# The extra rows of an expert in pieces: the products behind their own branches, set between the steps of the main products

## The chip, the cores and the metric

The kernel runs on one core of a Trainium2 chip. The metric is the device time of one execution in microseconds (us). The engines are TensorE (PE in the profile, with PEld for its weight loads and PEq for its sequencer), VectorE (DVE), ScalarE (ACT), GpSimd (POOL) and SyncE (SP); DMA queues bring in the weights.

## The reference, cut to what matters

One decoder layer for 1024 tokens of width 1024: a mixer of three branches, a LayerNorm, and then a mixture of 16 experts, of which each token uses two. The change touches only the experts:

```python
D_MODEL = 1024
SEQ = 1024
N_EXPERTS = 16
TOP_K = 2
D_EXPERT = 512
...
# for every expert e and the tokens that the router gave it
h = silu(x @ w1[e]) * (x @ w3[e])      # 1024 -> 512
y = h @ w2[e]                          # 512 -> 1024
# weighted by the router and added to the token's row
```

With 1024 tokens and two experts each, an expert has 128 tokens on average, and some have more.

## The kernel before, in words

The first 1380 us of the span are the mixer and the router. The experts follow, one after the other, in a loop that is unrolled in the program. An expert has a **main part**: its first 128 tokens, one per partition. Their rows are gathered (`fetch`, tile xg), transposed on PE (`turn_a`: tile pxg, then ACT copies it to xgH and DVE makes xgL), multiplied by w1 and w3 in eight contraction steps (`layer1`, `mm_pair`, L1580, tiles ph), put through silu (`act`: ACT's tanh and two DVE operations make mhh), transposed (`turn2`: phT, mhH on ACT, mhL on DVE) and multiplied by w2 in four contraction steps (`layer2`, L1580, tiles py). ACT scales the result (mo, L1812) and POOL adds it to the rows in memory. Each weight tile of 128 rows and 1024 columns is split into two parts before it is used: a copy on ACT (L1634) and a subtraction on DVE (L1635), 12 such splits for an expert. A split is planned at the end of every step (`ws.step`), which also frees buffers and starts further loads.

The tokens above 128 are the **extra rows**, in groups m = 0 to 3 of 32. A value that is loaded from the router's counts (`count_of`, L1698) decides which groups there are. Each use of PE for them stands in a nest of four branches (`per_part`): the first group is computed when the count is over 128, the second, inside the first, when it is over 160, and so on. There are four stages with such a nest on PE: `part_x` transposes the gathered extra rows (then ACT copies them: xmT), `part_1` is the product with w1 and w3 (all eight contraction steps, 32 matmuls for a group, which the profile shows as 64), `part_act` is silu (mhm on ACT, two operations on DVE, no branch), `part_h` transposes (then ACT copies: hmT), `part_2` is the product with w2 (16 matmuls, shown as 32), and `part_y` multiplies by the router's weight on DVE (mom, no branch) and adds to memory from POOL. xmT, hmT, mhm and mom are made for all groups in every expert, whether it has extra rows or not. The stages write and read one tile `bank` in PSUM, whose half 0:256 of a group takes part_1's result and hT, and whose half 256:512 takes xT and part_2's result. The extra rows' products use the weight tiles as they were loaded, before the split, so that the loaded tiles can be given back (`ws.dropped`) only after them.

In the kernel before, a nest of part_1 or part_2 has a label, and a hint instruction some steps ahead of it (`ahead`, L1713) gives PE's sequencer the address that the branch will go to.

The order on PE, DVE and ACT is that in which the program is written. In the loop over experts e and steps c = 0 to 11, the steps 0 to 7 are layer1 of expert e, the steps 8 to 11 layer2 of expert e-1; after each step come the stages that a table (`AT`, `AT0` for the first expert, `LAST` for the last two) names for this step, and then `ws.step`. In a row (2, "part_1", 0) the numbers are the step and the expert counted from e.

## Time and profile before

| | us |
|---|---|
| median of three runs | 1901.77 (1892.07 to 1903.71) |
| the profiled execution | 1905.58 |
| its span | 1903.7 |
| experts in it, from about 1385 to 1864 us | 479 |

In a row of the trace a time in brackets is the idle time of the engine ahead of the row and what released it. "issue" is idle time for which the profile shows no wait, "PEq L1703" an instruction of PE's sequencer on the line of the branches. Consecutive instructions with the same operands are one row with their count.

### The profile page before, as it was taken

The page shows a single profiled execution, that of the slowest core. Times are in us where ns is not written, and L with a number is a line of the kernel's source. Part 1 is how long each engine was busy: PE and PEld are TensorE (multiplying, and loading weights), DVE is VectorE, ACT ScalarE, POOL GpSimd, SP SyncE. Part 2 cuts the span into 40 slices and gives each one's busy share as a digit, 9 for nine tenths or more (in the row PEclk, how much of TensorE's full clock was granted, in tenths as well). Part 3 has the DMA queues.
Part 4 walks back from the last instruction along what each step waited for, and adds up shares of the span by engine and source line. Part 5 has one row for each costly group of instructions (what it writes and reads, how often), then busy time and mean ns, then how long its engine had stood idle before and what let it go on. Part 6 is the DMA issues. An engine that isn't in the chain of part 4 may idle for free. (4 is left out here: it accounts for less than half of the span.)

```text
span 1903.7 us, 28756 instructions
## 1 busy us (share of the span) xinstructions
PE 1707.9 (90%) x10550; PEld 1433.5 (75%) x10550; DVE 1147.4 (60%) x2108; ACT 693.7 (36%) x1157; POOL 426.8 (22%) x434
## 2 busy tenths in 40 slices
PE   6996999999999999999999999999557978899782
PEld 5975988899998888888777778899545656677551
DVE  7699645544454442534476756735854547899666
ACT  6311322212212222435344532312133436688553
POOL 3186021113211103542110100000142213111115
PEclk9998999999999999999999999999779989999886
DMA  5232534233423233543200255482566768999835
GB/s 174 89 110 111 175 104 123 92 118 91 117 86 98 79 108 113 164 128 106 90 19 18 72 175 191 144 202 101 215 142 204 218 193 254 334 339 360 269 96 200
DMA packets 225790, 286.52 MB, mean 151 GB/s; under 512 B 48494, under 2 KB 153960, under 8 KB 225608
## 3 DMA queue, kind: packets, MB, share of 16 engines
q1 hardware_dynamic: 216936, 259.10, 42.2%
q0 software_dynamic: 8672, 24.94, 5.2%
q8 instruction: 120, 1.97, 0.4%
q14 instruction: 62, 0.51, 0.1%
HBM read 214.81 MB, written 69.17 MB: 149 GB/s over the span
## 5 line engine op out<-in xcount | busy, mean ns | idle before, releaser
L365 PE MATMUL psp<-xH,wh 128*128 128x512 f32 x704 | 286.3, 407 | 18.8 <-ACT ci L519 18.8
L366 PE MATMUL psp<-xL,wh 128*128 128x512 f32 x704 | 275.9, 392 | 3.8 <-DVE xL L234 2.3
L367 PE MATMUL psp<-xH,wl 128*128 128x512 f32 x704 | 277.2, 394 | 0.0
L365 PEld LDWEIGHTS psp<-xH,wh 128*128 128x128 f32 x704 | 133.3, 189 | 44.5 <-ACT ci L519 20.1
L365 PE MATMUL psp<-wh,xH 128*128 128x256 f32 (+1 forms) x576 | 166.2, 288 | 0.0
L367 PE MATMUL psp<-wh,xL 128*128 128x256 f32 (+1 forms) x576 | 162.9, 283 | 0.0
L366 PE MATMUL psp<-wl,xH 128*128 128x256 f32 (+1 forms) x576 | 162.9, 283 | 0.0
L366 PEld LDWEIGHTS psp<-xL,wh 128*128 128x128 f32 x704 | 133.4, 190 | 30.6 <-DVE xL L234 2.9
L367 PEld LDWEIGHTS psp<-xH,wl 128*128 128x128 f32 x704 | 132.8, 189 | 29.5
L1580 PE MATMUL ph<-wl,xgH 128*128 128x512 f32 x274 | 90.7, 440 | 32.0 <-issue 20.8
L365 PEld LDWEIGHTS psp<-wh,xH 128*128 128x128 f32 x576 | 110.9, 193 | 0.2
L366 PEld LDWEIGHTS psp<-wl,xH 128*128 128x128 f32 x576 | 110.9, 193 | 0.1
L367 PEld LDWEIGHTS psp<-wh,xL 128*128 128x128 f32 x576 | 110.9, 192 | 0.0
L351 DVE TENSOR_TENSOR wl<-wr,wh 128x1024 fp32r<-128x1024 f32 (+1 forms) x62 | 81.9, 1340 | 41.8 <-ACT wh L350 29.9
L1580 PEld LDWEIGHTS ph<-wl,xgH 128*128 128x128 f32 x274 | 55.2, 211 | 49.3 <-issue 31.3
L350 ACT ACTIVATE wh<-wr 128x1024 fp32r<-128x1024 f32 (+1 forms) x62 | 64.0, 1047 | 64.6 <-PE psp L366 40.6
L365 PE MATMUL pwo<-woh,mH 128*128 128x256 f32 x256 | 74.7, 292 | 1.6 <-DVE xs L2188 1.6
L365 PE MATMUL pbr<-yH,brh 128*128 128x512 f32 x192 | 75.5, 393 | 0.6 <-DMA ya<-ay 0.6
L366 PE MATMUL pbr<-yL,brh 128*128 128x512 f32 x192 | 75.5, 393 | 0.0
L367 PE MATMUL pbr<-yH,brl 128*128 128x512 f32 x192 | 75.3, 392 | 0.0
L367 PE MATMUL pwo<-woh,mL 128*128 128x256 f32 x256 | 73.1, 285 | 0.0
L366 PE MATMUL pwo<-wol,mH 128*128 128x256 f32 x256 | 73.0, 285 | 0.0
(855 smaller groups left out, 4137.0 us busy)
## 6 DMA issues: line engine op xcount, KB each, us to landing
wl<-in_moe_w_dram SPq DMA_DIRECT2D x126, 256.0 KB
wr<-in_w_in_dram SPq DMA_DIRECT2D x60, 512.0 KB
xs<-in_moe_w_dram SPq DMA_DIRECT2D x82, 256.0 KB
wl<-in_moe_w_dram SPq DMA_DIRECT2D x34, 512.0 KB
gates<-gt SPq DMA_DIRECT2D x24, 512.0 KB
mgt<-gates SPq DMA_DIRECT2D x48, 256.0 KB
we<-in_moe_w_dram SPq DMA_DIRECT2D x48, 256.0 KB
we<-in_moe_w_dram SPq DMA_DIRECT2D x18, 512.0 KB
```

The source lines that it names most:

```text
L350: k.nc.scalar.activation(h, raw, AF.Copy)
L351: k.nc.vector.tensor_sub(l, raw, h)
L365: k.nc.tensor.matmul(out, aH, bH, start=start, stop=False)
L366: k.nc.tensor.matmul(out, aH, bL, start=False, stop=False)
L367: k.nc.tensor.matmul(out, aL, bH, start=False, stop=stop)
L1580: k.nc.tensor.matmul(ps, xL if p == 2 else xH, wl if p == 1 else wh, start=first and p == 0, stop=last and p == 2)
```

## The change

`part_1` and `part_2` each take two contraction steps at a call (`STEP`) instead of all. part_1 is called four times for an expert and part_2 twice; each call is a nest of four branches of its own, with the accumulation in PSUM going on from call to call. The labels and hints are gone. The tables place the calls between the steps of the main products; so part_act moves from step 1 to step 8 of the expert's own iteration (before part_x of the next expert), part_h from 4 to 10, the first half of part_2 from step 3 of the next iteration to step 11 of the expert's own, and part_y from step 5 to 3.

```diff
-    def per_part(e, fn, eng=nc.tensor, name=None):
+    def per_part(e, fn, eng=nc.tensor):
         count = count_of(e, eng)
         with ExitStack() as st:
             for m in range(NM):
-                label = f"{name}_{e}_{m}" if name else None
-                st.enter_context(tc.If(count > P + 32 * m, label=label))
-                if name and m + 1 < NM:
-                    ahead(e, name, m + 1)
+                st.enter_context(tc.If(count > P + 32 * m))
                 fn(m)
-
-    def ahead(e, name, m=0):
-
-        tc.mark_branch_hint_location(f"{name}_{e}_{m}", hint=count_of(e, nc.tensor) > P + 32 * m, engines=[ENG.PE])
...
+        def turns(e, name, n):
+
+            i = A[e].turn[name] = A[e].turn.get(name, -n) + n
+            return range(i, i + n)
+
         def part_1(e):
-            a = A[e]
-            keys = [(e, 1, c) for c in range(KD)]
+            a, cs = A[e], turns(e, "1", STEP)
+            keys = [(e, 1, c) for c in cs]
             w = [t.rearrange("p (i q n) -> p i q n", i=2, q=4) for t in ws.whole(keys)]
 
             def mul(m):
-                for c, t in enumerate(w):
+                for c, t in zip(cs, w):
...
         def part_2(e):
-            a = A[e]
-            keys = [(e, 2, c) for c in range(4)]
+            a, cs = A[e], turns(e, "2", STEP)
+            keys = [(e, 2, c) for c in cs]
             w = list(ws.whole(keys))
...
-AT = ((0, "part_1", 0), (0, "turn2", -1), (0, "ahead_2", -1), (1, "part_act", 0), (3, "turn_a", 1), (3, "part_2", -1),
-      (3, "ahead_1", 1), (4, "part_h", 0), (5, "part_y", -1), (7, "act", 0),
-      (8, "part_x", 1), (9, "fetch", 2))
+AT = ((0, "turn2", -1), (1, "part_2", -1), (2, "part_1", 0), (3, "turn_a", 1), (3, "part_y", -1), (4, "part_1", 0),
+      (6, "part_1", 0), (7, "act", 0), (7, "part_1", 0), (8, "part_act", 0), (8, "part_x", 1), (9, "fetch", 2),
+      (10, "part_h", 0), (11, "part_2", 0))
+STEP = 2
```

AT0 and LAST are rewritten in the same sense. On PE, before, after step 0 of a late expert (ph are the main product's tiles; the three other groups of the nest, left out here, follow in the same form):

```order
L1580 MATMUL ph_18417<-wl_18319,xgL 128x512
L1580 MATMUL ph_18418<-wl_18319,xgL 128x512
L1703 COMPARE_AND_BRANCH
L1713 REGISTER_ALU
L2464 BRANCH_PREFETCH_HINT
L1835 MATMUL bank<-wl_17844,xmT 32x256 x4
L1835 MATMUL bank<-wl_17873,xmT 32x256 x4
L1835 MATMUL bank<-xs_17905,xmT 32x256 x4
L1835 MATMUL bank<-wl_17918,xmT 32x256 x4
L1835 MATMUL bank<-wl_17935,xmT 32x256 x4
```

On PE in the changed kernel, a late expert from the end of step 7's main product on (L1833 is part_1's product, L1698 the load of the next expert's count; the other groups of the nest are left out):

```order
L1580 MATMUL ph_17899<-we_18014,xgL 128x512
L1580 MATMUL ph_17900<-we_18014,xgL 128x512
L1703 COMPARE_AND_BRANCH
L1833 MATMUL bank<-wl_17498,xmT 32x256 x4
L1833 MATMUL bank<-wl_17547,xmT 32x256 x4
...
L1703 UNCONDITIONAL_BRANCH x5
L1580 MATMUL py<-xs_18053,mhH 128x512 x2
L1580 MATMUL py<-wl_18054,mhH 128x512 x2
L1580 MATMUL py<-xs_18053,mhL 128x512 x2
L1698 TENSOR_LOAD cnt
```

The fourth piece stands after the last step of layer1 and one step of layer2 ahead of the load of the next count, where one nest of eight steps stood after step 0.

On ACT, before, from the main part's tanh (mhh) to the extra rows' tanh of the next iteration (mhm); xmT is that of the next expert:

```order
L1571 ACTIVATE mhh<-ph_17938 128x512 [waits PE_49]
L1634 ACTIVATE wl_18319<-wl_17844 128x1024 [waits DMAHW4_49,DMAHW3_49,DVE_49]
L1703 UNCONDITIONAL_BRANCH x3
L1824 ACTIVATE xmT<-bank 128x1024 [waits DVE_49,PE_49]
L1634 ACTIVATE we_18348<-wl_17873 128x1024 [waits DMAHW6_49,DMAHW5_49,Activation_49]
L1634 ACTIVATE xs_18380<-xs_17905 128x1024 [waits DMAHW7_49,DMAHW0_49,DVE_49]
L1634 ACTIVATE we_18393<-wl_17918 128x1024 [waits DMAHW2_49,DMAHW1_49,DVE_49]
L1812 ACTIVATE mo<-py,oh 128x512 [waits DMASW3_49,PE_49]
...
L1566 ACTIVATE mhH<-phT 128x512 [waits PE_49]
L1634 ACTIVATE wl_18578<-wl_18103 128x1024 [waits DMAHW6_49,DMAHW5_49]
L1571 ACTIVATE mhm<-bank 128x512
```

On ACT in the changed kernel, the same stretch:

```order
L1571 ACTIVATE mhh<-ph_17899 128x512 [waits PE_49]
L1634 ACTIVATE we_18213<-wl_17746 128x1024 [waits DMAHW4_49,DMAHW3_49]
L1571 ACTIVATE mhm<-bank 128x512 [waits PE_49]
L1703 UNCONDITIONAL_BRANCH x2
L1817 ACTIVATE xmT<-bank 128x1024 [waits DVE_49,PE_49]
L1634 ACTIVATE we_18255<-wl_17788 128x1024 [waits DMAHW6_49,DMAHW5_49]
L1634 ACTIVATE wl_18287<-xs_17820 128x1024 [waits DMAHW7_49,DMAHW0_49]
L1703 UNCONDITIONAL_BRANCH
L1848 ACTIVATE hmT<-bank 128x512 [waits PE_49]
L1634 ACTIVATE wl_18310<-xs_17843 128x1024 [waits DMAHW2_49,DMAHW1_49]
L1703 UNCONDITIONAL_BRANCH
L1805 ACTIVATE mo<-py,oh 128x512 [waits DMASW3_49,PE_49]
```

The extra rows' tanh has moved to just ahead of xmT, with which it shares the tile bank, and hmT from step 4 of the next iteration to the stretch between xmT and mo. On DVE, in the changed kernel, what stands against these rows (the subtraction is that of the split ahead of mhm on ACT, and of the first one behind xmT):

```order
L1572 SCALAR_TENSOR_TENSOR mhh<-mhh,ph_17899 128x512 [waits Activation_49]
L1573 TENSOR_TENSOR mhh<-mhh,ph_17900 128x512 [waits DVE_49,PE_49]
L1635 TENSOR_TENSOR xs_18214<-wl_17746,we_18213 128x1024 [waits DMAHW4_49,DMAHW3_49,Activation_49]
L1572 SCALAR_TENSOR_TENSOR mhm<-mhm,bank 128x512 [waits Activation_49]
L1573 TENSOR_TENSOR mhm<-mhm,bank 128x512 [waits DVE_49]
L1703 UNCONDITIONAL_BRANCH x2
L1635 TENSOR_TENSOR wl_18256<-wl_17788,we_18255 128x1024 [waits DMAHW6_49,DMAHW5_49,Activation_49]
```

All five operations now follow each other there, and it is the last one on mhm whose count the DVE wait of xmT names.

## Rows read from the trace of the kernel before

**Rows 1.** The page: busy time of each engine, the granted clock of PE and the share of the DMA engines in 40 slices, and the queue that fetches instructions (packets, MB, share).

```profile
PE 1707.9 (90%) x10550; PEld 1433.5 (75%) x10550; DVE 1147.4 (60%) x2108; ACT 693.7 (36%) x1157; POOL 426.8 (22%) x434
...
PEclk9998999999999999999999999999779989999886
DMA  5232534233423233543200255482566768999835
...
q8 instruction: 120, 1.97, 0.4%
```

**Rows 2.** Busy time in each stretch of the experts: the stretch and its length, busy us of PE, PEld, DVE, ACT and POOL with the number of instructions, the granted clock, the share of the DMA engines, GB/s.

```profile
1385.00:1436.00 51.00, 35.32 (x289) 23.61 (x289) 22.90 (x44) 18.85 (x24) 24.58 (x21) 0.80 0.59 128
1436.00:1515.00 79.00, 64.97 (x536) 45.74 (x537) 39.33 (x40) 34.03 (x42) 17.31 (x11) 0.94 0.67 200
1515.00:1590.00 75.00, 60.77 (x446) 43.29 (x445) 40.73 (x42) 36.41 (x46) 13.33 (x8) 0.91 0.68 207
1680.00:1740.00 60.00, 55.49 (x247) 42.66 (x248) 56.37 (x60) 49.48 (x62) 11.17 (x6) 1.00 0.99 340
1740.00:1800.00 60.00, 48.60 (x250) 36.48 (x249) 42.85 (x45) 38.16 (x49) 11.17 (x7) 0.90 0.92 308
```

**Rows 3.** The line of the branches: its instructions on PE's sequencer over the whole span (ns at least, median, at most), the engines that waited for it (us, times), and the same instructions between 1680 and 1740 us.

```profile
L1703 PEldq COMPARE_BRANCH  x140: 65/189/6161, 1390.7 to 1843.1; - x140
...
  PE ph L1580: 32.5, 19
...
  PE phT L1555: 21.3, 10
...
L1703 PEldq COMPARE_BRANCH  x12: 252/412/442, 1682.3 to 1738.3; - x12
```

**Rows 4.** PE's instructions in order of time around long gaps: start, duration, line, operands, count and the idle time ahead.

```profile
1403.50 2.06 PE L1580 MATMUL ph<-wl,xgH 128*128 128x512 f32 x4 [5.38 <-issue]
...
1408.76 1.09 PE L1580 MATMUL ph<-wl,xgH 128*128 128x512 f32 x4
...
1449.78 2.06 PE L1580 MATMUL ph<-wl,xgH 128*128 128x512 f32 x4 [5.48 <-issue]
...
1474.64 0.69 PE L1555 MATMUL phT<-ident,mhh 128*128 128x128 f32 x2 [4.00 <-PEq L1703]
...
1550.56 0.66 PE L1555 MATMUL phT<-ident,mhh 128*128 128x128 f32 x4 [3.49 <-PEq L1703]
...
1771.98 0.78 PE L1580 MATMUL ph<-xs,xgH 128*128 128x512 f32 x1 [4.00 <-PEq L1703]
...
1796.70 0.69 PE L1555 MATMUL phT<-ident,mhh 128*128 128x128 f32 x2 [4.78 <-PEq L1703]
```

**Rows 5.** PE's transposes of turn2, one for each iteration: the first, two in the late experts without extra rows, and the last.

```profile
1436.73 0.44 PE L1555 MATMUL phT<-ident,mhh 128*128 128x128 f32 x2 [1.37 <-PEq L1703]
1679.92 0.41 PE L1555 MATMUL phT<-ident,mhh 128*128 128x128 f32 x2
1700.46 0.41 PE L1555 MATMUL phT<-ident,mhh 128*128 128x128 f32 x2
1863.84 0.66 PE L1555 MATMUL phT<-ident,mhh 128*128 128x128 f32 x2 [6.33 <-DVE mhh L1573]
```

**Rows 6.** PE around branches that are not long: the end of a nest that was computed (1489.48, 1490.18), and a nest that was jumped over (between 1687.77 and 1688.55).

```profile
1489.48 0.27 PE L1848 MATMUL bank<-ident,mhm 128*128 128x128 f32 x1
1490.18 0.73 PE L1580 MATMUL ph<-we,xgH 128*128 128x512 f32 x2 [0.42 <-PEq L1703]
...
1687.31 0.62 PE L1580 MATMUL ph<-wl,xgH 128*128 128x512 f32 x2
1687.77 0.62 PE L1580 MATMUL ph<-we,xgL 128*128 128x512 f32 x2
1688.55 0.94 PE L1580 MATMUL ph<-wl,xgH 128*128 128x512 f32 x3
```

**Rows 7.** part_1's products from 1385 to 1904 us, grouped: operands, count, busy us and mean ns of one, idle time ahead. (None of them stands between 1590 and 1740 us.)

```profile
L1835 PE MATMUL bank<-wl,xmT 128*32 128x256 f32 x328 | 23.4, 380 | 0.1
L1835 PE MATMUL bank<-xs,xmT 128*32 128x256 f32 x248 | 18.4, 397 | 0.0
L1835 PE MATMUL bank<-we,xmT 128*32 128x256 f32 x128 | 9.4, 381 | 0.0
```

**Rows 8.** ACT in a late expert without extra rows, from the main part's tanh on.

```profile
1713.25 0.60 ACT L1571 ACTIVATE mhh<-ph 128x512 f32<-128x512 f32 x1 [0.80 <-PE ph L1580]
1713.74 1.05 ACT L1634 ACTIVATE wl<-wl 128x1024 fp32r<-128x1024 f32 x1
1714.96 1.03 ACT L1824 ACTIVATE xmT<-bank 128x1024 f32<-128x1024 f32 x1 [0.17 <-PEq L1703]
```

**Rows 9.** DVE in the same expert.

```profile
1707.43 1.28 DVE L1562 TENSOR_TENSOR xgL<-pxg,xgH 128x512 fp32r<-128x512 f32 x2
...
1711.72 1.22 DVE L1869 TENSOR_TENSOR mom<-bank,oh 128x1024 f32<-128x1024 f32 x1
...
1715.12 0.68 DVE L1572 SCALAR_TENSOR_TENSOR mhh<-mhh,ph 128x512 f32<-128x512 f32 x1
1715.91 0.69 DVE L1573 TENSOR_TENSOR mhh<-mhh,ph 128x512 f32<-128x512 f32 x1
1716.52 1.22 DVE L1635 TENSOR_TENSOR wl<-wl,wl 128x1024 fp32r<-128x1024 f32 x1
```

## The prediction

> **What bounds the kernel now.** The experts fill the time from 1385 us on, and the change touches nothing ahead of it, so I read the stretches first [rows 2]. They show three regimes. Between 1680 and 1740 us no expert has extra rows: DVE is busy 56.37 of 60 us (94%), PE 55.49, ACT 49.48 (82%), and the DMA engines' share is 0.99. One iteration, from one transpose of turn2 to the next, takes 1700.46 - 1679.92 = 20.5 us [rows 5]. From 1436 to 1590 us DVE falls to 50 to 54%, from 1740 to 1800 to 71%, PE to some 81% in both, and the granted clock from 1.00 to between 0.90 and 0.94. Here PE sets the pace, and it stands idle in pieces.

> A second estimate of the same loss: from the first to the last transpose of turn2 there are 15 iterations and 427.1 us [rows 5], 119.6 us more than 15 clean ones. part_1's 704 records, 64 for a group, are 11 groups in 51.2 us busy [rows 7]; part_2, with half the records, adds about 26. About a quarter of that 77 lies before 1436 us; some 60 us of the 119.6 is work, and 60 remain. [...]

> **The change, part by part.** (1) *Shorter jumps.* A piece of part_1 is a quarter of the nest, one of part_2 a half, so every jump over such a nest shrinks to about 128 products and weight loads (64 of each). The 53.8 us of waits contain ordinary ends of nests, which stay: an end costs 0.42 us [rows 6], and with some 20 such ends among the 29 waits about 45 us are stalls. The restart at the low clock adds about 1 us for four products [rows 4], 1 to 2 us at some four to eight gaps, 8 together. I take -52 us; 40 and 65 are the ends, the lower if some stalls remain, the upper from the 60 above plus the stalls before 1436 us. The late experts without extra rows gain nothing here, since none of their branches is long [rows 3].

> (2) *More nests.* An expert has six product nests instead of two. In an expert with extra rows (0 to 5, 14 and 15: eight) four more are entered and left, 0.42 us and about 0.1 for the branch each [rows 6, 3]: 2.0 us, 16 in all if nothing covers it. I take 12, since part of it falls into waits below. In the eight others a jumped nest shows as 1688.55 - 1687.77 = 0.78 us, where the pair ahead took 1687.77 - 1687.31 = 0.46 [rows 6], so 0.3 us; four are 1.2 us, against PE's idle share of 8% (1.5 us an iteration). It is hidden as long as DVE is the bound, so 0, at most 8 for all. The hints that go away are short instructions on PE and give back less than that.

> [...]

> (3) *xmT behind mhm.* part_act now stands right ahead of part_x, in the same tile. xmT on ACT, made in every expert, waits for DVE's second operation on mhm. DVE runs 1715.12 - 1713.25 = 1.87 us behind ACT at mhh [rows 8, 9]. From ACT's mhh on, DVE needs 1.87 + 0.79 + 0.61 for mhh, 1.13 for the split between and 1.37 for mhm (as for mhh), about 5.8 us; ACT gets to xmT after 0.49 + 0.95 + 0.5 = 1.9. ACT stands for up to 3.9 us, and its idle share of 18% is 3.7 us an iteration. Behind it are queued the next splits, hmT and mo. DVE then waits for xmT (1.03) and one split (1.05), 2.1 us, of which its own idle time (6%, 1.2 us) can take a part. So an iteration without extra rows grows by 0.9 to 2.1 us; I take 1.5, eight times, 12 us (bounds 6 and 17).

> (4) *part_x on PE behind mhm.* Where the next expert has extra rows (1 to 5, 14, 15: seven), PE's transposes wait for the same operation. From the fourth piece's end it is 0.42 + 0.60 + 0.68 + 0.69 us, up to 1.2 more for a split on DVE ahead, 2.4 to 3.6; one step of layer2 (1.4 us, six products at 0.46 for two [rows 6]) covers a part. 1 to 2.2 us of idle PE, queued behind: the rest of layer2. Seven times 2 is 14 us (bounds 5 and 18). Before, part_act had seven steps between itself and part_x.

> (5) *Pieces behind mom.* part_y stands at step 3 behind turn_a, and mom reads the bank that the next piece of part_1 writes. On DVE, mom follows the two xgL: 0.60 (ACT's xgH) + 1.28 + 1.22 = 3.1 us [rows 9] behind PE's transposes; PE has one step, 1.4 us, to do before the second piece. 1.7 us in eight experts, 14 us (bounds 0, if DVE is ahead, and 20).

> (6) *Buffers.* The loaded tiles of part_1 come free at steps 2 to 7 and not at 0, those of part_2 earlier; about two tiles more are held. With a DMA share of 0.99 a late load could be felt in the clean stretch; 0 to 8 us, I take 2. The count's load moves from step 3 to 8 and costs PE the same.

> Sum: -52 + 12 + 0 + 12 + 14 + 14 + 2 = +2 us. The profiled execution took 1905.58 us, 3.8 above the median of 1901.77; the forecast is against the median, **1904 us**, no change that a measurement here can tell (about 1%, 19 us).

> **The rivals.** *Faster: the waits are covered.* Terms 4 and 5 are bounds on a chain taken alone; in experts with extra rows DVE is busy only some 53% of the time [rows 2], so it may have no lag at all, and the spread pieces give ACT and DVE work in parallel. With 5 us for each of these, 6 for term 3 and 8 for term 2, the sum is -52 + 24 = -28: 1874 us. Against it: the waits are in program order on three engines, and none of them can be overtaken.

> *Slower: two jumps in quick succession.* The pieces at steps 1 and 2, and those at 6 and 7, have one main step between, 1.4 us. If two jumps in that time land past what the sequencer has loaded, the second stalls as a long jump does now, 3.49 to 5.48 us [rows 4], less what has passed: about 3. There are 32 pairs; if a third of them is hit, 11 stalls, 33 us: 1937 us. The hints that could have prevented it are gone. It decides against the change from about six stalls on. [...]

> *The change doesn't take the stalls away.* If any jump past a 16 KB portion stalls, however short, then the 48 product nests that the eight clean experts jump, now mostly hinted, would stall in perhaps half the cases: 24 x 3.5 = 84 us, with half of term 1 lost: about 2010 us. Against it: the jumps over part_x and part_h, which have no hint, are among the 12 of the late stretch, the shortest of which took 252 ns and none over 442 [rows 3].

> **How the numbers follow.** Forecast 0.41; covered waits 0.27; stalls of pairs 0.25; stalls that stay 0.07. The range has to leave out the last and the tails of the two others: 1868 to 1942 us. Its ends are the bounds of terms 1 to 6, where most can't go to their ends together, with the two middle rivals inside. Faster by over 1% (below 1882.8): most of the first rival, with a little of the forecast's tail, 0.28. Slower by over 1% (above 1920.8): most of the second, all of the third, 0.32. Within 1%: 0.40.

> **What would show it.** Term 1: branches on PE's sequencer over 1 us are gone, and the clock in the stretches before 1590 us is near 1.00. Term 3: ACT waits for DVE's mhm ahead of xmT, 2 to 4 us in each iteration, and the clean iteration takes 21.4 to 22.6 instead of 20.5 us. Terms 4 and 5: PE waits for mhm ahead of part_x and for mom ahead of part_1. The pairs: branches of 2 to 6 us at the pieces of step 2 and 7. The forecast is wrong if the clean iteration stays at 20.5 us, or if the long branches are still there.

## The result, and the profile of the changed kernel

The changed kernel takes 1919.8 us (median of 16 runs, 1912.67 to 1926.33), the kernel before 1900.84 in 16 runs: a ratio of 1.0098, 95% interval 1.0081 to 1.0116. It is 1% slower, and the interval is clear of 1. The forecast was 1904, no change that a measurement could tell, and the range 1868 to 1942.

The page of the changed kernel gives the granted clock and the queue of instructions (packets, MB, share), as in [rows 1]:

```profile
PEclk9998999999999999999999999999789999999996
...
q8 instruction: 132, 2.16, 0.5%
```

Behind the two slices in which the router ends, the clock has no dip until the last slice, and 12 more portions of instructions were fetched. Three of the stretches of [rows 2], columns as there:

```profile
1436.00:1515.00 79.00, 66.22 (x501) 42.90 (x499) 41.37 (x43) 36.67 (x46) 16.06 (x12) 0.96 0.70 213
1515.00:1590.00 75.00, 63.73 (x528) 40.19 (x528) 39.71 (x41) 34.40 (x43) 13.86 (x9) 0.98 0.70 207
...
1680.00:1740.00 60.00, 52.02 (x217) 36.77 (x216) 48.03 (x48) 43.78 (x55) 6.73 (x5) 0.97 0.92 297
```

Between 1680 and 1740 us, where no expert has extra rows, DVE was busy 56.37 us before and is busy 48.03 now, and the share of the DMA engines has gone from 0.99 to 0.92. Neither is as full any more in this clean stretch (iterations without extra rows); waits have come in.

Where the time went is read from the transposes of turn2. Two of the kernel before, then three of the changed one:

```profile
1635.04 0.41 PE L1555 MATMUL phT<-ident,mhh 128*128 128x128 f32 x2 [1.46 <-PEq L1703]
1762.29 0.41 PE L1555 MATMUL phT<-ident,mhh 128*128 128x128 f32 x2 [0.15 <-PEq L1703]
```

```profile
1427.43 0.41 PE L1555 MATMUL phT<-ident,mhh 128*128 128x128 f32 x1
1637.56 0.44 PE L1555 MATMUL phT<-ident,mhh 128*128 128x128 f32 x2 [1.01 <-ACT mo L1805]
1780.36 0.44 PE L1555 MATMUL phT<-ident,mhh 128*128 128x128 f32 x2 [0.95 <-ACT mo L1805]
```

1635.04 and 1637.56 are the seventh, behind all the work of experts 0 to 5: +2.5 us. (At the first the changed kernel is 9.3 us earlier, 1427.43 against 1436.73 [rows 5], but that is no gain: there part_1's products of expert 1, 128 records and some 9 us by [rows 7], stand behind it, and in the kernel before ahead of it.) The thirteenth are at 1762.29 and 1780.36: six iterations without extra rows cost 15.6 us more, 2.6 each. At the end the spans differ by 14.4; the profiled execution of the kernel before was 4.7 us above its median, so the traces show 14 of the 19 us. Against the kernel before, then, the experts with extra rows come out nearly even, and the loss lies in those that have none, which the change was not about.

The branches, from 1385 to 1590 us and from 1590 to 1800, before and then changed:

```profile
L1703 PEldq COMPARE_BRANCH  x76: 65/174/5585, 1390.7 to 1589.3; - x76
...
L1703 PEldq COMPARE_BRANCH  x45: 70/365/6161, 1593.1 to 1796.5; - x45
```

```profile
L1703 PEldq COMPARE_BRANCH  x151: 65/176/453, 1388.8 to 1586.2; - x151
...
L1703 PEldq COMPARE_BRANCH  x82: 65/219/4927, 1591.0 to 1799.4; - x82
```

Before 1590 us, in the experts with extra rows, the longest branch is now 453 ns; the stalls of [rows 4] that lie there are gone, as term 1 said. Behind 1590 us they are not: of the branches over 0.5 us the changed kernel has 17 with 44 us together, 15 of them between 1590 and 1770 us (the kernel before had 19 with 69 us, 8 with 25 us between 1590 and 1770). The iterations between 1680 and 1740 us, free of them before [rows 3], have them now, at the pieces of steps 2, 4, 6 and 7 and at part_2's of step 1. During one of them, 1696.4 to 1700.4 us, one portion of instructions came in:

```profile
q8 instruction: 1, 0.02, 1.6%
```

It is so in 13 of the 17 (the other four took 1.0 to 1.1 us): in the times of the queue's packets a portion ends while the branch runs, and the branch ends 1.2 to 1.5 us later. In the kernel before the same holds for 16 of the 19. By these times the long branches wait for instructions, for which the prediction had found no row.

One clean iteration of the changed kernel, ACT, then DVE, then PE:

```profile
1716.48 1.09 ACT L1561 ACTIVATE xgH<-pxg 128x512 fp32r<-128x512 f32 x2 [1.98 <-PE pxg L1550]
...
1725.31 0.60 ACT L1571 ACTIVATE mhm<-bank 128x512 f32<-128x512 f32 x1 [0.71 <-PEq L1703]
1728.09 1.03 ACT L1817 ACTIVATE xmT<-bank 128x1024 f32<-128x1024 f32 x1 [2.17 <-DVE mhm L1573]
...
1730.09 1.22 DVE L1635 TENSOR_TENSOR wl<-wl,we 128x1024 fp32r<-128x1024 f32 x1 [2.10 <-ACT we L1634]
...
1722.63 0.63 PE L1580 MATMUL ph<-we,xgL 128*128 128x512 f32 x2
1725.48 0.70 PE L1580 MATMUL py<-xs,mhH 128*128 128x512 f32 x2 [2.23 <-PEq L1703]
```

Two things happen within 8 us: PE stands 2.23 us at the fourth piece, and ACT stands 2.17 us ahead of xmT until DVE has finished mhm, after which DVE stands 2.10 us until ACT has made xmT and a split. Earlier in the iteration ACT had waited 1.98 us for PE's transposes of the next rows. Which of the two sets the pace can't be read here. The experiments take them apart.

### The profile page after: what moved, and what is told of

It reads as the page before. It is cut to its first block, busy times and chain, and to the rows that moved or that the text cites. A ratio compares the mean times of both kernels' runs of the same rounds, so it can differ in the third digit from the quotient of the medians.

```text
span 1918.1 us, 28852 instructions
## 1 busy us (share of the span) xinstructions
PE 1717.0 (90%) x10550; PEld 1413.2 (74%) x10550; DVE 1150.7 (60%) x2108; ACT 693.6 (36%) x1157; POOL 415.0 (22%) x434
## 5 line engine op out<-in xcount | busy, mean ns | idle before, releaser
L365 PEld LDWEIGHTS psp<-xH,wh 128*128 128x128 f32 x704 | 133.3, 189 | 43.8 <-ACT ci L519 19.3
L1580 PE MATMUL ph<-wl,xgH 128*128 128x512 f32 x258 | 80.8, 416 | 22.3 <-PEq L1703 17.3
L1580 PEld LDWEIGHTS ph<-wl,xgH 128*128 128x128 f32 x258 | 44.1, 189 | 48.8 <-issue 26.8
```

Source lines behind the costliest of these rows:

```text
L365: k.nc.tensor.matmul(out, aH, bH, start=start, stop=False)
L1580: k.nc.tensor.matmul(ps, xL if p == 2 else xH, wl if p == 1 else wh, start=first and p == 0, stop=last and p == 2)
```

## The experiments

Each was timed against the kernel before on its chip (1898.5 to 1900.6 us); the ratios are to that.

**Without hints.** The kernel before, all labels and hints out:

```diff
-            per_part(e, mul, name="p1")
+            per_part(e, mul)
...
-            per_part(e, mul, name="p2")
+            per_part(e, mul)
...
-AT = ((0, "part_1", 0), (0, "turn2", -1), (0, "ahead_2", -1), (1, "part_act", 0), (3, "turn_a", 1), (3, "part_2", -1),
-      (3, "ahead_1", 1), (4, "part_h", 0), (5, "part_y", -1), (7, "act", 0),
+AT = ((0, "part_1", 0), (0, "turn2", -1), (1, "part_act", 0), (3, "turn_a", 1), (3, "part_2", -1),
+      (4, "part_h", 0), (5, "part_y", -1), (7, "act", 0),
```

> The kernel before with its labels and hints taken out and nothing else. If the hints are what keeps the late experts' jumps at 0.4 us (theory of the prediction: a jump over a long nest has to fetch its target), two jumps in each of some eight clean iterations go from 0.44 to 3 to 6 us: 1935 to 1965 us, and the 20.5 us iterations become 25 to 29. Rival, the hints only cost issue time and the late jumps are short for another reason: 1895 to 1902 us, iterations still at 20.5 us.

1916.09 us, 1.0089 (1.0057 to 1.0122). Branches from 1690 to 1740 us and three transposes of turn2, the first of them the seventh:

```profile
L1703 PEldq COMPARE_BRANCH  x9: 217/4212/6620, 1686.3 to 1735.7; - x9
```

```profile
1618.98 0.52 PE L1555 MATMUL phT<-ident,mhh 128*128 128x128 f32 x3
...
1666.89 0.41 PE L1555 MATMUL phT<-ident,mhh 128*128 128x128 f32 x2 [3.01 <-PEq L1703]
1691.82 0.52 PE L1555 MATMUL phT<-ident,mhh 128*128 128x128 f32 x3 [2.48 <-PEq L1703]
```

The clean iteration is 24.9 us where it was 20.5, with one or two branches of 3.8 to 6.6 us in each. Where the late experts' jumps were short, it was because of the hints. The iterations nearly fit the first theory (25 to 29 us), but the total fell below its 1935, for the kernel is earlier at the seventh transpose, 1618.98 us against 1635.04 before: the hints cost some 16 us where the experts have extra rows.

**Hints in the changed kernel.** One main step ahead of each nest, first branch only, in experts 1 to 13:

```diff
+    def ahead(e, name):
+        i = A[e].turn.get(name, -STEP) + STEP
+        tc.mark_branch_hint_location(f"p{name}{i}_{e}_0", hint=count_of(e, nc.tensor) > P, engines=[ENG.PE])
...
+AT = ((0, "turn2", -1), (0, "ahead_2", -1), (1, "part_2", -1), (1, "ahead_1", 0), (2, "part_1", 0), (3, "turn_a", 1), (3, "part_y", -1),
+      (3, "ahead_1", 0), (4, "part_1", 0), (5, "ahead_1", 0),
+      (6, "part_1", 0), (6, "ahead_1", 0), (7, "act", 0), (7, "part_1", 0), (8, "part_act", 0), (8, "part_x", 1), (9, "fetch", 2),
+      (10, "part_h", 0), (10, "ahead_2", 0), (11, "part_2", 0))
```

> The changed kernel with a hint one main step ahead of each of its six product nests (first branch of the nest only). Theory S, the loss is the stalls that are left (branches over 0.5 us sum to 44 us in the trace of the changed kernel): they mostly go, 1885 to 1900 us, clean iterations near 21 us. Theory O, the loss is the order (xmT behind mhm, pieces behind mom): within 5 us of the changed kernel, 1915 to 1925 us, although the long branches are fewer.

1937.58 us, 1.0198 (1.0163 to 1.0233): slower by 18 us than without them, which neither theory had. From 1590 to 1800 us:

```profile
L1703 PEldq COMPARE_BRANCH  x75: 68/245/6451, 1594.5 to 1798.9; - x75
```

The longest branch is 6451 ns where it was 4927, and those over 0.5 us take 67 us in all where they took 44. Hints one step ahead of their branches made some stalls longer here and prevented few, so this run says nothing of what an iteration without stalls would take.

**part_x ahead of part_act.**

```diff
-      (6, "part_1", 0), (7, "act", 0), (7, "part_1", 0), (8, "part_act", 0), (8, "part_x", 1), (9, "fetch", 2),
+      (6, "part_1", 0), (7, "act", 0), (7, "part_1", 0), (8, "part_x", 1), (8, "part_act", 0), (9, "fetch", 2),
```

> The changed kernel with part_x and part_act exchanged, so that xmT on ACT and the next expert's transposes on PE no longer wait for DVE's mhm; all nests stay. Theory O: 15 to 30 us back, 1890 to 1905 us, clean iterations at 21 to 22 us. Theory S: 1912 to 1920 us, long branches as many as in the changed kernel.

1917.37 us, 1.0088 (1.0060 to 1.0116): 2 us better, within what this can tell. A clean iteration, PE and ACT:

```profile
1698.77 0.71 PE L1580 MATMUL py<-we,mhH 128*128 128x512 f32 x2 [2.82 <-PEq L1703]
...
1700.53 1.03 ACT L1817 ACTIVATE xmT<-bank 128x1024 f32<-128x1024 f32 x1 [3.25 <-PEq L1703]
```

ACT no longer waits for mhm ahead of xmT, but 3.25 us for PE, which comes late from a stall at the fourth piece. By itself this reads as a win for theory S. It isn't: the next kernels show that the wait was covered, not small.

**Both together.** The two edits above.

> Both together, the hints and the exchange. If the two losses add: 1865 to 1885 us. If one covers the other: the better of the two alone, about 1890 to 1905 us.

1929.76 us, 1.0167 (1.0131 to 1.0203). It lies between the two, since the hints of this place are a loss by themselves (18 us); neither forecast came true, and it doesn't decide.

**Without the product nests**, the changed kernel and the kernel before (hints out). Both leave the extra rows' products of part_1 and part_2 out:

```diff
-            per_part(e, mul)
             ws.dropped(keys)
```

> The changed kernel with the product nests of part_1 and part_2 left out (the extra rows' products aren't computed; part_x, part_h, the ACT and DVE operations and their order stay). To be read against the next kernel, which is the same for the order before. Theory O (the order costs by itself): its clean iterations are 1 to 2 us longer than the other's, 12 to 30 us in all. Theory S (what is lost is lost in the jumps): both within 5 us and clean iterations at 20.3 to 20.8 us in both.

> The kernel before with its hints and the product nests of part_1 and part_2 left out (the extra rows' products aren't computed). Some 77 us of products and all long branches go, of which the DMA bound gives part back: 1770 to 1800 us, clean iterations at 20.3 to 20.8 us.

1850.33 us in the changed order, 0.9737 (0.9718 to 0.9756), and 1792.72 in the order before, 0.9443 (0.9423 to 0.9462). The same work, with no branch over 0.5 us in either, differs by 57.6 us. A clean iteration in the changed order, ACT, DVE and PE:

```profile
1656.44 1.09 ACT L1561 ACTIVATE xgH<-pxg 128x512 fp32r<-128x512 f32 x2 [2.06 <-PE pxg L1550]
...
1668.05 1.03 ACT L1817 ACTIVATE xmT<-bank 128x1024 f32<-128x1024 f32 x1 [3.47 <-DVE mhm L1573]
...
1670.05 1.23 DVE L1635 TENSOR_TENSOR wl<-wl,we 128x1024 fp32r<-128x1024 f32 x1 [2.10 <-ACT we L1634]
...
1649.59 0.66 PE L1555 MATMUL phT<-ident,mhh 128*128 128x128 f32 x4 [2.89 <-ACT mo L1805]
...
1673.02 0.66 PE L1555 MATMUL phT<-ident,mhh 128*128 128x128 f32 x4 [2.82 <-ACT mo L1805]
```

and two transposes in the order before:

```profile
1634.46 0.49 PE L1555 MATMUL phT<-ident,mhh 128*128 128x128 f32 x3
1653.73 0.49 PE L1555 MATMUL phT<-ident,mhh 128*128 128x128 f32 x3
```

23.4 us against 19.3. The chain closes on itself: ACT waits 3.47 us for mhm, so mo is late; PE's transposes of turn2 write a buffer that mo reads (phT and py share a tag), and wait 2.82 us for it; so PE comes late to the transposes of the next rows, and ACT waits 2.06 us for those. Theory O holds, and the price is about twice the most that it expected (57.6 us against 30, 4.1 an iteration against 2). A part of it may be the clock: from 1600 to 1700 us the granted clock is 0.93 in the changed order and 1.00 in the order before.

**The exchange without the nests.** The edit of part_x ahead of part_act, and the nests out.

> The changed kernel with part_x ahead of part_act and the product nests of part_1 and part_2 left out (the extra rows' products aren't computed). Without the exchange and without the nests a clean iteration took 23.3 us, in the order before 19.3. If xmT behind mhm is the whole price of the order: 19.3 to 20.5 us an iteration, 1795 to 1815 us. If another place of the order has as much part in it (hmT ahead of mo, mo ahead of the transposes of turn2): 21.5 to 23 us, 1825 to 1845 us.

1805.28 us, 0.9508 (0.9481 to 0.9536).

```profile
1645.34 0.44 PE L1555 MATMUL phT<-ident,mhh 128*128 128x128 f32 x2 [0.75 <-ACT mo L1805]
1665.14 0.44 PE L1555 MATMUL phT<-ident,mhh 128*128 128x128 f32 x2 [0.78 <-ACT mo L1805]
```

19.8 us an iteration: the exchange gives 45 of the 57.6 us back, and the wait for mo falls from 2.82 to 0.78. So part_x behind part_act (in these iterations xmT behind mhm) is most of the order's price, and it shows in full only where no stall covers it (45 us here, 2 us with the nests).

**One group in a nest.** The exchange, and in each product nest the first group alone; the products of the other groups are left out:

```diff
-            for m in range(NM):
+            for m in range(groups):
                 st.enter_context(tc.If(count > P + 32 * m))
...
-            per_part(e, mul)
+            per_part(e, mul, groups=1)
```

> The changed kernel with part_x ahead of part_act, and only the first group's products in each nest of part_1 and part_2 (those of the second and third group, which two experts have, aren't computed: 3 of the 11 groups, some 16 us of PE). The nests and branches are as many as before, each a quarter as long. If the stalls come from the length of code that is jumped over and has to be fetched past: no branch over 1 us or few, clean iterations at 20 to 21 us, against 24 with the full nests and 19.8 without nests; 1835 to 1855 us. If they come from the number of branches: clean iterations still at 23 to 25 us, 1880 to 1900 us.

1854.48 us, 0.9770 (0.9728 to 0.9813), in the range of the first theory. Its branches from 1590 to 1800 us and two transposes:

```profile
L1703 PEldq COMPARE_BRANCH  x92: 65/208/443, 1591.7 to 1792.7; - x92
```

```profile
1657.17 0.49 PE L1555 MATMUL phT<-ident,mhh 128*128 128x128 f32 x3
1678.61 0.49 PE L1555 MATMUL phT<-ident,mhh 128*128 128x128 f32 x3
```

As many nests as in the changed kernel, a quarter as long: no branch over 443 ns, and 21.4 us an iteration, between the 19.8 without nests and the 24 with full ones (1707.1 - 1683.1 in the kernel with the exchange). In these two kernels the length of the code that is jumped over makes the stalls, not the number of branches (443 ns at most here, 5337 ns with the exchange and full nests); six short jumps cost 1.6 us an iteration. Whether the length of one jump counts, or all the code that is passed in an iteration, this run doesn't separate. The portions of instructions from 1600 to 1760 us, in the changed kernel, with one group, and without nests:

```profile
q8 instruction: 27, 0.44, 1.2%
```

```profile
q8 instruction: 13, 0.21, 0.5%
```

```profile
q8 instruction: 6, 0.10, 0.3%
```

**The pieces where the whole products stood.** All four of part_1 at step 0, both of part_2 at step 3, no hints:

```diff
+AT = ((0, "part_1", 0), (0, "part_1", 0), (0, "part_1", 0), (0, "part_1", 0), (0, "turn2", -1), (1, "part_act", 0), (3, "turn_a", 1), (3, "part_2", -1), (3, "part_2", -1),
+      (4, "part_h", 0), (5, "part_y", -1), (7, "act", 0),
+      (8, "part_x", 1), (9, "fetch", 2))
```

> The pieces, each behind its own nest and without hints, but all four of part_1 at step 0 and both of part_2 at step 3, where the whole products stood (the tables of the kernel before). Against the kernel before without hints (1916 us) it tells the price of four more nests in a row, against the changed kernel that of the moves. If the jumps in a row stall as the one long jump does, and an executed nest costs 0.5 us: 1918 to 1930 us. If short jumps are cheap wherever they stand: 1890 to 1900 us, clean iterations near 21 us.

1950.51 us, 1.0282 (1.0233 to 1.0330), worse than both theories and 34 us above the kernel before without hints. The portions fetched are nearly as many, 132 against 129 over the span, so more fetching isn't the reason; what makes jumps in a row so dear stays open. One row of PE shows a loss that no branch carries, and the queue has one portion in the gap, from 1755.9 to 1757.3 us:

```profile
1758.76 0.80 PE L1580 MATMUL ph<-we,xgL 128*128 128x512 f32 x1 [3.71 <-issue]
```

```profile
q8 instruction: 1, 0.02, 6.0%
```

In the middle of a main step PE has nothing to do for 3.71 us, and no wait is shown. It goes on 1.5 us behind the end of the portion, as the long branches do, so by these times it waited for instructions here too. The sum over long branches (64 us here) leaves such a loss out. The changed kernel, with the pieces spread, is 31 us shorter in spite of its order.

**Hints of the kernel before, fewer.** First the outer ones alone:

```diff
-                if name and m + 1 < NM:
-                    ahead(e, name, m + 1)
```

> The kernel before with the hints of the outermost branch of each nest alone (those inside a nest, for the next group, are taken out). Without any hints the first five iterations (experts with extra rows) were 21 us shorter than before and the late ones 4.4 us longer each. If the inner hints are what costs in the experts with extra rows and the outer ones what helps in the late ones: 1875 to 1888 us. If the outer hint is harmful there too (it names the address inside the nest as the one to come): 1893 to 1902 us, as before.

1907.01 us, 1.0038 (1.0013 to 1.0063), above both ranges. At the seventh transpose the kernel is at 1617.9 us, as early as without any hint (1619.0), so it was the inner hints, for the next group of a nest, that cost 16 us there; the late experts took the gain back. Branches of two neighbouring clean iterations, in each part_2's, part_h's, part_x's and part_1's:

```profile
L1703 PEldq COMPARE_BRANCH  x4: 261/498/8458, 1697.5 to 1718.9; - x4
```

```profile
L1703 PEldq COMPARE_BRANCH  x4: 261/459/540, 1725.1 to 1740.1; - x4
```

The same hint at the same place (part_2's, three steps ahead) is followed by a branch of 8.5 us in one iteration and by none over 0.54 in the next. Then with the hint of the next part_1 at step 10 instead of 3:

```diff
-      (3, "ahead_1", 1), (4, "part_h", 0), (5, "part_y", -1), (7, "act", 0),
-      (8, "part_x", 1), (9, "fetch", 2))
+      (4, "part_h", 0), (5, "part_y", -1), (7, "act", 0),
+      (8, "part_x", 1), (9, "fetch", 2), (10, "ahead_1", 1))
```

> The kernel before with outer hints alone, and the hint of the next part_1 at step 10 instead of step 3, so that no other nest stands between the hint and its branch. With the hint at step 3 some of the late experts' jumps at step 0 still took 4 to 6 us. If what lies between makes the sequencer lose the target: these go, clean iterations at 20.5 us from expert 6 on, 1875 to 1890 us. If two steps are too little time ahead: 1900 to 1915 us.

1902.54 us, 1.0026 (1.0007 to 1.0046), in the range of the second theory; clean iterations of 26 us up to 1720 us. part_1's branch of one late iteration, with the hint at step 3 and then at step 10:

```profile
L1703 PEldq COMPARE_BRANCH  x1: 523/523/523, 1718.9 to 1718.9; - x1
```

```profile
L1703 PEldq COMPARE_BRANCH  x1: 4681/4681/4681, 1716.4 to 1716.4; - x1
```

With the hint nine steps ahead and other nests between, part_1's jumps from 1600 to 1745 us took at most 0.54 us; two steps ahead, with no nest between, all six take 3.6 to 5.6 us. So the nests between hint and branch are not the reason, and two steps were too few. (The stalls that this run was to take away were part_2's, whose hint it left in place.) The distance isn't all: in the kernel before, with the hint of part_1 at step 3 too, three of its late jumps took 4.3 to 5.2 us. What else decides whether a hint works stays open.

**Halves with hints three steps ahead**, with part_x ahead of part_act, meant to beat both:

```diff
+AT = ((0, "turn2", -1), (1, "part_2", -1), (1, "ahead_1", 0), (3, "turn_a", 1), (3, "part_y", -1), (4, "part_1", 0),
+      (4, "ahead_1", 0), (7, "act", 0), (7, "part_1", 0), (8, "part_x", 1), (8, "part_act", 0), (9, "fetch", 2),
+      (10, "part_h", 0), (10, "ahead_2", 0))
+STEP = 4
```

> A version meant to beat both: part_x ahead of part_act; part_1 in two pieces of four steps (steps 4 and 7), part_2 whole at step 1 of the next iteration, each first branch hinted three main steps (4 us) ahead. If three steps are enough for the hint: clean iterations at 20.5 us, experts with extra rows 2 us shorter than in the changed kernel for the three nests less: 1865 to 1885 us. If the hints miss as those one step ahead did: 1905 to 1925 us.

1903.76 us, 1.0019 (1.0000 to 1.0038): just under its second forecast: some 16 us better than the changed kernel, no better than the kernel before.

```profile
L1703 PEldq COMPARE_BRANCH  x49: 75/372/7540, 1592.3 to 1796.5; - x49
```

Hints miss here too. No version that computes everything beat the kernel before.

## Why the prediction was right, and where it wasn't

The time fell inside the range, and the balance was of the kind that the prediction gave: stalls gone where experts have extra rows, given back to new waits. But the forecast was +2 us, no change, and it is +19, clear of the noise. By the prediction's own signs it held in part only: long branches are still there (17 with 44 us), and a clean iteration takes 142.8 / 6 = 23.8 us, not 21.4 to 22.6. That the number came so near is in part luck, since its errors had opposite signs. Put together, the medians show how the two prices cover each other:

| order | without product nests | with them | the nests' price |
|---|---|---|---|
| before, no hints | 1792.7 | 1916.1 | 123 |
| before, with hints | | 1900.8 | 108 |
| changed | 1850.3 | 1919.8 | 69 |
| changed, part_x first | 1805.3 | 1917.4 | 112 |

The order of the change costs 57.6 us where PE has no stalls. The nests, whose price holds some 77 us of products by the prediction's estimate, cost 108 to 123 us where the order is good, and 69 where the waits of the order already hold PE up. The exchange, which takes most of the order's waits away, returns 45 us without the nests and 2 us with them.

*Term 1, -52 us, held for the stalls in sum, not for the restart and not for the late experts.* The stalls before 1590 us went, and the clock rose (0.94 and 0.91 to 0.96 and 0.98 in the two stretches from 1436 us). For PE's waits at the branches the prediction counted 53.8 us in 29 and left out those of py, 3.8 us in 8; the 57.6 us in 37 waits are now 45.7 in 76. Three rows of the changed kernel, then py's of the kernel before and its gaps ahead of ph that are put down to "issue":

```profile
  PE ph L1580: 26.3, 47
...
  PE py L1580: 18.8, 28
  PE phT L1555: 0.6, 1
```

```profile
  PE py L1580: 3.8, 8
```

```profile
PE ph L1580 <- issue: 22.2, 8, 5.5
```

With all gaps of PE put down to "issue", 23.6 us before and 1.8 now, its idle time at the branches fell by 34 us; the 45 us of stalls less the 12 of term 2 are 33. (The long branches themselves fell by 25 us in sum, but a branch runs in part while PE still works: that of 1721.6 us took 3.5, and PE stood 2.23.) The low clock behind a stall is in the trace of the kernel before (a granted clock of 0.50 from 1403.4 to 1408.7 us and from 1449.8 to 1451.8, and of 0.99 from 1408.7 to 1410.0). But the 8 us of the restart did not come: PE's busy time for the same 10550 instructions rose from 1707.9 [rows 1] to 1717.0 us. Why, no run shows.

The place was wrong too. That the late experts have no long branches was read from 60 us of them [rows 3]; from 1590 to 1770 us eight took 25 us. And where the branches were short, that had a cause which the change removes, the hints (two for an expert without extra rows); without hints the same iterations take 24.9 us. The prediction also took the hints for short instructions that give back little. They are short (54 of them, a median of 35 ns), but without them the old order is at the seventh transpose 18.6 us ahead of the changed kernel (1618.98 and 1637.56, one profiled execution of each), and loses only 3.7 of it in the next six iterations. So, against the old order without hints, the pieces in their new places are a loss in the experts that they were made for. The share of each wait in it no run shows.

*The rival of the pairs was half right.* Stalls came back, of 1 to 5 us, but not at pairs alone: also at steps 4 and 6, two main steps behind the last nest. The length of the code counts, as one group in a nest shows (no branch over 443 ns). The prediction put these stalls down to instructions that have to be fetched, and the portions agree: one came in during 13 of the 17 long branches, and from 1600 to 1760 us 27 were fetched in the changed kernel, 13 with one group in a nest and 6 without nests. Which jumps make PE wait for a portion no row shows. Term 1 needed jumps of a quarter of the old length to be free of such stalls, and in the clean stretch some two in six were not (15 long branches in 7 to 8 iterations).

*Term 2's 0 for the jumped nests* was too low: with one group a nest, six jumps cost 21.4 - 19.8 = 1.6 us an iteration (one group against none). For the four that the change adds that is 1.1 us, some 9 us in eight iterations, a little over the upper bound of 8.

*Term 3, 12 us, had the waits right and the sum wrong.* Estimated were ACT's wait of up to 3.9 us and DVE's of 2.1; measured without nests 3.47 and 2.10. But the prediction stopped there and let DVE's idle time take a part. The wait goes on, from mo to the transposes of turn2, from these to the transposes of the next rows, and back to ACT. An iteration grew by 4.1 us, not 1.5. In the changed kernel itself waits and stalls overlap: with both, a clean iteration takes 23.8 us on the average, hardly more than the 23.4 without nests, and 2.6 more than before.

*Terms 4 and 5* had the right waits. In the changed kernel, over all experts (in total, times, longest):

```profile
PEld bank L1833 <- DVE mom L1867: 10.5, 6, 1.8
...
PEld bank L1813 <- DVE mhm L1573: 6.3, 5, 2.9
...
ACT xmT L1817 <- DVE mhm L1573: 16.0, 6, 3.0
ACT xmT L1817 <- PEq L1703: 24.5, 10, 3.6
```

Behind mom the sum had 14 us and the trace has 10.5; behind mhm it had 14 and the trace has 6.3. The last two rows are the two sides of term 3: of its 16 times ACT waited for mhm at xmT in six and for PE in ten. So the errors had opposite signs: 17 us too much gain in term 1 for the restart, 11 us too much cost in terms 4 and 5, too little in term 3 and in the jumped nests of term 2. The balance was nearer than its parts. Term 6, 2 us, no run shows by itself.

## What to carry to other kernels

Where a step is moved, follow its new wait through every engine until it comes back to the first; a wait that closes on itself is paid in every iteration, and idle time of the engines in the loop doesn't cover it (here 4.1 us in each). A short time in the profile (the late branches here: at most 442 ns between 1680 and 1740 us with the hints, up to 6620 ns there without) may hang on instructions that the change removes, so ask what keeps it short before calling it untouched. And when two losses stand at the same place, removing one may show nothing (2 us for the exchange here, and 45 without the nests): take each away in a kernel where the other is absent.

## What the runs showed that was not expected

The hints helped in the late experts (20.5 against 24.9 us), and those inside the nests cost 16 us up to the seventh transpose; hints one step ahead of their branches lost 18 us in all. The same hint worked in one iteration and not in the next, with branches of 8458 and 540 ns at most. And PE stood 3.71 us in the middle of a main step with no branch and no wait shown (the pieces where the whole products stood), and went on 1.5 us behind the portion that came in.
